# One scan instead of two for the diagonal tiles of stick-breaking attention, with zeros and the identity as the added operand

## The chip, the cores and the metric

The kernel runs on one core of one Trainium2 chip, as one launch for the whole layer. The metric is the time of an execution on the device, in microseconds. The core has five engines that run on their own queues and wait for each other: TensorE (PE in the profile, its weight loads PEld), VectorE (DVE), ScalarE (ACT), GpSimd (POOL) and SyncE (SP), which here issues the DMA transfers.

## What is computed

One layer of a hybrid encoder over a prompt of 2048 frames and 64 frames of a running stream, in fp32. The layer has one input projection of the normalised input; a recurrent branch (RG-LRU), a pooling branch and stick-breaking attention of four heads of 64; one output projection; and a feed-forward part (SwiGLU). The part that matters here is the attention:

```python
def stick_breaking(q, k, v, q_pos, k_pos):
    z = jnp.einsum("bqhd,bkhd->bhqk", q, k)
    mask = k_pos[None, :] < q_pos[:, None]
    nl = jnp.where(mask, jnp.log1p(jnp.exp(z)), 0.0)
    ...                       # surv[k] = sum of nl[j] over j >= k
    attn = jnp.where(mask, jnp.exp(z - surv), 0.0)
    return jnp.einsum("bhqk,bkhd->bqhd", attn, v)
```

With om = sigmoid(-z) = 1 / (1 + exp(z)), the product C[k] of om[j] over the keys j from k to the last one before the query is what is left of the stick, and attn[k] = C[k+1] - C[k]. The kernel computes C and multiplies it with differences of neighbouring rows of v, which were stored beforehand.

## The kernel before, in words

The prompt is worked through in four groups of 512 frames. For each group there are dense units (input projections in three fp32r products, the recurrent branch, pooling, queries, keys and values of the next group) and attention units. The program merges both into one list by hand-set weights (the lists o0, o1, o3 and the numbers alag and aspan in line 3), marks the attention units with a priority, and a scheduler lays out the order of each engine's instructions when the program is built, by these priorities and by when it reckons operands ready. So two neighbouring lines of code needn't be neighbours in an engine's queue. Then come the output projection and the feed-forward part.

An attention unit of group g takes one head, one block c of 512 keys (c from g down to 0) and two tiles of 128 queries. ATT_units (L673) loads queries, keys and differenced values with SP, from DRAM scratch that the earlier units wrote (kscr, qscr, vscr). For each of the two tiles it calls att_qtile (L647): PE multiplies queries by keys into the PSUM tile z (L650, L651); ACT overwrites z by the sigmoid (L653); DVE makes C in SBUF by scans from the last column to the first. A scan computes state = om * state + added, column after column. Back in ATT_units PE transposes C in pieces of 128 columns (L705), ACT and DVE split the transposes into a high and a low part (L706, L707), and PE multiplies both by the values into av. att_out (L665) adds the value of the query's own frame and stores.

Off the diagonal (c < g) a tile has 512 columns and one scan (L661) with zeros as the added operand (one column of zeros, zero1, broadcast) and the carry of the block to its right as its start. On the diagonal (c = g) the tile of query tile qt has (qt + 1) * 128 columns. There the last dg = 128 columns have a scan of their own (L657) with the reversed identity as the added operand and 0.0 as its start: the state stays zero for the keys after the query, is set to one at the query's own position and is a product from there on. A second scan (L661) goes on over the remaining w - dg columns, from that scan's last value. The sample's tile (ATT_sample, L723) has 64 queries and 320 columns, with dg = 64, once for each head.

The identity comes by DMA in X_first (L836), and shift_consts (L394) makes DVE constants from it. X_first also computes the first group's row statistics on PE from sums that DVE and POOL add up (L864). Keys go through fin_ (L366): DVE scales them (L368) and splits them (L315), SP stores them to kscr (L324), and the attention of the next group loads them (L685). The recurrent branch has scans of its own (L579).

Of the kernel before, what the change touches and what calls it, by code (L numbers as in the profile page):

```python
# [3 lines left out]
def prm(n,d):  # L4
    return type(d)(PRM.get(n,d))
# [7 lines left out]
F32 = mybir.dt.float32  # L13
# [3 lines left out]
ALU = mybir.AluOpType  # L17
# [4 lines left out]
P = 128  # L22
# [11 lines left out]
GW = 512  # L34
# [15 lines left out]
def hybrid_layer(ctx: ExitStack, tc: tile.TileContext, x_all, x_t, w_in, w_out, w_gu, w_dn, par, gates, poolw,  # L50
                 gn2, ident_in, cache_k, cache_v, y, new_k, new_v, o_conv, o_lru, o_pool):
    nc = tc.nc
    act, dve, gp, pe, sp = nc.scalar, nc.vector, nc.gpsimd, nc.tensor, nc.sync
# [23 lines left out]
    def mm(out, lhsT, rhs, start, stop):  # L77
        pe.matmul(out, lhsT, rhs, start=start, stop=stop)  # L78
# [35 lines left out]
    ident = cp.tile([P, P], F32, name="ident")  # L114
# [279 lines left out]
    def shift_consts():  # L394
        dve.tensor_scalar(dm[:, 0:1], ident[:, 0:1], -1.0, None, ALU.mult)
        dve.tensor_tensor(dm[:, 1:], ident[:, :P - 1], ident[:, 1:], ALU.subtract)
        dve.tensor_copy(em[:, 0:1], ident[:, P - 1:])
        sp.dma_start(clast, cache_v[PAST - 1:PAST, :])
# [244 lines left out]
    pa = s_att.enter_context(tc.tile_pool(name="pa", bufs=2, side="right"))  # L643
    zero1 = pa.tile([P, 1], F32, name="zero1", bufs=1)
    gp.memset(zero1, 0.0)

    def att_qtile(q2, n, K, w, dg, carry):  # L647

        z = psum.tile([P, GW], F32, name="z", tag="z", bufs=prm("nz", 2))
        mm(z[:n, :w], q2[:, 0, :], K[:, :w], True, False)  # L650
        mm(z[:n, :w], q2[:, 1, :], K[:, :w], False, True)  # L651
        om = z
        act.activation(om[:n, :w], z[:n, :w], AF.Sigmoid, scale=-1.0)  # L653
        C = pa.tile([P, GW], F32, name="C", bufs=prm("b_C", 5))
        if dg:

            dve.tensor_tensor_scan(C[:n, w - dg:w][:, ::-1], om[:n, w - dg:w][:, ::-1], ident[:n, :dg][:, ::-1], 0.0,  # L657
                                   ALU.mult, ALU.add)
            w, carry = w - dg, C[:n, w - dg:w - dg + 1]
        if w:  # L660
            dve.tensor_tensor_scan(C[:n, :w][:, ::-1], om[:n, :w][:, ::-1], zero1[:n].to_broadcast([n, w]), carry,  # L661
                                   ALU.mult, ALU.add)
        return C, C[:n, 0:1]

    def att_out(av, h, n, q2, vsrc, dst):  # L665
# [7 lines left out]
    def ATT_units(g):  # L673
        us = []
        for h in range(NH):
            st = {}
            for c in range(g, -1, -1):
# [11 lines left out]
                def u(pr, h=h, c=c, st=st, ld=ld):  # L689
                    if pr == 0:  # L690
                        ld()
                        if c == g:
                            st["av"] = psum.tile([P, GW], F32, name="av", tag="av", bufs=1)
                    q2, av, K, V = st["q"], st["av"], st["K"], st["V"]
                    aTh = pa.tile([P, 4, 256], F32R, name="aTh", bufs=prm("b_aTh", 2))
                    aTl = pa.tile([P, 4, 256], F32R, name="aTl", bufs=prm("b_aTl", 2))
                    for qq in range(2):
                        qt = pr * 2 + qq
                        nk = 4 if c < g else qt + 1
                        dg = P if c == g else 0  # L700
                        at, st["carry"][qt] = att_qtile(q2[:, :, qt * P:(qt + 1) * P], P, K, nk * P, dg,
                                                        st["carry"][qt])
                        tp = ps_a()
                        for kt in range(nk):
                            pe.transpose(tp[:, kt, :], at[:, kt * P:(kt + 1) * P], ident)  # L705
                        act.copy(aTh[:, :nk, qq * P:(qq + 1) * P], tp[:, :nk, :])  # L706
                        dve.tensor_tensor(aTl[:, :nk, qq * P:(qq + 1) * P], tp[:, :nk, :],  # L707
                                          aTh[:, :nk, qq * P:(qq + 1) * P], ALU.subtract)
                    nkt = 4 if c < g else 2 * pr + 2
                    for kt in range(nkt):  # L710
                        q0 = P if c == g and kt == 2 * pr + 1 else 0
                        o = av[:, pr * 256 + q0:pr * 256 + 256]
                        mm(o, V[:, kt, :], aTh[:, kt, q0:], c == g and kt == 0 and pr == 0, False)
                        mm(o, V[:, kt, :], aTl[:, kt, q0:], False, c == 0 and kt == nkt - 1 and pr == 1)
                    if c == 0 and pr == 1:
                        att_out(av, h, GW, q2, vtscr[g], mix[g])
# [6 lines left out]
    def ATT_sample(h):  # L723
        n, w = NS, PAST + NS
        q2 = pa.tile([P, 2, GW], F32R, name="q2", bufs=prm("b_q2", 2))
        for e in range(2):
            sp.dma_start(q2[e * HD:e * HD + HD, :, :n].bitcast(F32), qscr_s[h])
        K = pa.tile([P, GW], F32R, name="K", bufs=prm("b_K", 2))
        sp.dma_start(K[:, :w].bitcast(F32), kscr_s[h])
        V = pa.tile([P, 4, P], F32R, name="V", bufs=prm("b_V", 2))  # L730
        sp.dma_start(V[:, :2, :].bitcast(F32), vscr_s[:PAST, h, :].rearrange("(t p) e -> p t e", p=P))
        sp.dma_start(V[:NS, 2, :].bitcast(F32), vscr_s[PAST:, h, :])
        av = psum.tile([P, GW], F32, name="av", tag="av", bufs=1)
        at, _ = att_qtile(q2[:, :, :n], n, K, w, NS, 0.0)
        tp = ps_a()
        aTh = pa.tile([P, 4, 256], F32R, name="aTh", bufs=prm("b_aTh", 2))
        aTl = pa.tile([P, 4, 256], F32R, name="aTl", bufs=prm("b_aTl", 2))
        for kt, m in ((0, P), (1, P), (2, NS)):
            pe.transpose(tp[:m, kt, :n], at[:n, kt * P:kt * P + m], ident[:n, :n])
        for (m, a, b) in ((P, 0, 2), (NS, 2, 3)):  # L740
            act.copy(aTh[:m, a:b, :n], tp[:m, a:b, :n])
            dve.tensor_tensor(aTl[:m, a:b, :n], tp[:m, a:b, :n], aTh[:m, a:b, :n], ALU.subtract)
        for kt, m in ((0, P), (1, P), (2, NS)):
            mm(av[:, :n], V[:m, kt, :], aTh[:m, kt, :n], kt == 0, False)
            mm(av[:, :n], V[:m, kt, :], aTl[:m, kt, :n], False, kt == 2)
        att_out(av, h, n, q2, vtscr_s, mix_s)
# [68 lines left out]
    def X_first():  # L815
# [3 lines left out]
        for i in range(4):  # L819
# [10 lines left out]
            else:  # L830
# [4 lines left out]
        sp.dma_start(xs_, x_t[:, :, SEQ:].rearrange("k p t -> p k t"))  # L835
        sp.dma_start(ident, ident_in)  # L836
        shift_consts()
        acc = [psum.tile([P, 512], F32, name=t, tag=t, bufs=b) for t, b in
               (("tp", prm("ntp", 2)), ("tp", prm("ntp", 2)), ("z", prm("nz", 2)), ("z", prm("nz", 2)), ("av", 1))]
        sums = [pl.tile([P, SW], F32, name=t, tag=t, bufs=LB[t])[:, :GW] for t in ("r", "i")]  # L840
# [2 lines left out]
        for k in range(KD):  # L843
# [9 lines left out]
            w = slice((k % 4) * 256, (k % 4) * 256 + 256)  # L853
# [41 lines left out]
        for j, (ti, c0, n) in enumerate(toks(0)):  # L895
            with hp('ev'):
                ev_v(0, acc[j][:, :256], ti, c0, n, rss[:n, 0:1] if j == 4 else rs[1][:, j:j + 1])

    X_first()
    load_consts()  # L900
    if prm('cpos', 0) == 0:
# [475 lines left out]
```

## Time and profile before

| | us |
|---|---|
| median of three runs | 2429.84 |
| lowest and highest | 2428.33, 2432.44 |
| the profiled execution | 2430.59 |
| its span in the trace | 2428.8 |

| engine | busy us | share of the span |
|---|---|---|
| PE | 2315.6 | 95% |
| PEld | 2204.5 | 91% |
| DVE | 1561.7 | 64% |
| POOL | 1112.7 | 46% |
| ACT | 965.6 | 40% |

Busy times are read from the trace of one execution. The span is the trace's own length; the profiled execution's time is 1.8 us longer. Matmuls overlap in PE's pipeline, so that a busy PE isn't PE at its peak; the weight loads (PEld) show better how densely it is fed. The share of a whole span hides the stages: attention and the dense units run from 170 to 840 us, what follows is the output projection and the feed-forward part.

### The profile page before, as it was taken

Reading aid. Unit: us, or ns where it says so; the run is one execution under the profiler, and the core shown is the slowest. Engines: PE = TensorE matmul, PEld = TensorE weight load, DVE = VectorE, ACT = ScalarE, POOL = GpSimd, SP = SyncE. Lnnn points to the kernel's source line nnn. Section 1 sums busy time; section 2 is a strip of 40 time slices with the busy share of each in tenths; the row PEclk is TensorE's granted clock in tenths of the full one; section 3 lists DMA queues with packets and bytes.
Section 4 is the critical chain, followed back from the end, with each engine's and each line's share of the span. In section 5 each row is a group of like instructions: output and inputs, shape, how many; then the busy total and the mean of one; then the engine's idle time right before and its main releaser. Section 6 shows DMA issues by size and latency. Waiting matters only on the chain.

```text
span 2428.8 us, 38577 instructions
## 1 busy us (share of the span) xinstructions
PE 2315.6 (95%) x14230; PEld 2204.5 (91%) x14230; DVE 1561.7 (64%) x2514; ACT 965.6 (40%) x1804; POOL 1112.7 (46%) x818
## 2 busy tenths in 40 slices
PE   6987999999889989889999999999999999999999
PEld 6976778779678989889999999999999999999999
DVE  4568486796798644696676768655554655555455
ACT  4545364464565422233333343334333433333332
POOL 4533030131131133576565666656565765655552
PEclk8999999999999999999999999999999999999999
DMA  8986777656546354774343348633333563333332
GB/s 281 262 280 197 222 219 225 192 192 206 170 150 175 104 146 129 250 233 131 113 139 118 123 147 267 237 105 122 109 108 114 160 214 108 118 112 108 115 110 74
DMA packets 228478, 399.90 MB, mean 165 GB/s; under 512 B 37697, under 2 KB 99714, under 8 KB 220354
## 3 DMA queue, kind: packets, MB, share of 16 engines
q1 hardware_dynamic: 228290, 397.44, 52.6%
q8 instruction: 112, 1.84, 0.3%
q14 instruction: 76, 0.62, 0.1%
HBM read 300.81 MB, written 96.54 MB: 164 GB/s over the span
## 4 chain that ended last, share of the span: by engine, by line
PE 72%; DVE 12%; DMA 9%; issue 3%; ACT 2%; SPq 1%; POOL 1%; DVEq 0%; ACTq 0%; POOLq 0%
PE gu L78 33%; PE dn L78 20%; PE mm L78 14%; PE z L78 2%; PE av L78 2%; DVE C L661 1%; PE tp L705 1%; DMA rb<-xrow 1%; DMA kscr<-hl 1%; PE tp L78 1%; DVE xc L533 1%; DMA rbk<-row 1%; DMA x1all<-xr 1%; DMA wk<-w 1%; DVE al L1226 1%
## 5 line engine op out<-in xcount | busy, mean ns | idle before, releaser
L86 POOL TENSOR_TENSOR w<-x,w 128x512 fp32r<-128x512 f32 x462 | 640.7, 1401 | 509.7 <-ACT w L1103 478.4
L78 PE MATMUL dn<-ah,wd 128*128 128x352 f32 x2112 | 548.0, 324 | 5.4 <-ACT ah L1225 3.4
L78 PE MATMUL gu<-ht,w 128*128 128x352 f32 x2112 | 545.8, 323 | 7.3 <-DVE u L1180 7.1
L1103 ACT CAST w<-x 128x512 fp32r<-128x512 f32 x462 | 279.0, 619 | 521.2 <-PE gu L78 295.8
L78 PE MATMUL mm<-hTh,w 128*128 128x512 f32 (+3 forms) x1632 | 431.2, 342 | 13.7 <-DVE xr L1005 7.3
L78 PE MATMUL gu<-hb,w 128*128 128x352 f32 x1584 | 417.3, 325 | 9.0 <-DMA x<-in_w_gu 7.3
L1256 DVE TENSOR_TENSOR acc<-dn,acc 128x352 f32<-128x352 f32 x528 | 273.1, 522 | 217.5 <-PE dn L78 216.9
L78 PEld LDWEIGHTS dn<-ah,wd 128*128 128x128 f32 x2112 | 376.4, 189 | 7.6 <-ACT ah L1225 4.2
L78 PEld LDWEIGHTS gu<-ht,w 128*128 128x128 f32 x2112 | 375.1, 188 | 8.9 <-issue 5.9
L78 PE MATMUL dn<-al,wd 128*128 128x352 f32 x1056 | 342.4, 324 | 3.3 <-DVE al L1226 3.3
L78 PE MATMUL gu<-lt,w 128*128 128x352 f32 x1056 | 341.0, 323 | 0.0
L78 PEld LDWEIGHTS mm<-hTh,w 128*128 128x128 f32 x1632 | 290.2, 194 | 44.3 <-DVE xr L1005 8.5
L78 PEld LDWEIGHTS gu<-hb,w 128*128 128x128 f32 x1584 | 284.1, 189 | 11.1 <-ACT w L1103 9.5
L78 PE MATMUL mm<-hTl,w 128*128 128x512 f32 (+3 forms) x816 | 277.6, 341 | 0.8 <-DVE hTl L303 0.4
L78 PE MATMUL gu<-lb,w 128*128 128x352 f32 x792 | 257.1, 325 | 0.0
L86 POOL TENSOR_TENSOR wd<-x,wd 128x512 fp32r<-128x512 f32 x132 | 192.4, 1478 | 51.6 <-ACT wd L1244 51.6
L78 PEld LDWEIGHTS dn<-al,wd 128*128 128x128 f32 x1056 | 199.7, 189 | 4.5 <-DVE al L1226 4.5
L78 PEld LDWEIGHTS gu<-lt,w 128*128 128x128 f32 x1056 | 198.6, 188 | 0.0
L78 PEld LDWEIGHTS mm<-hTl,w 128*128 128x128 f32 x816 | 157.8, 193 | 15.7 <-issue 1.4
L661 DVE TENSOR_TENSOR_SCAN C<-z,C,zero 128x512 f32<-128x512 f32 (+4 forms) x148 | 160.6, 1087 | 13.9 <-ACT z L653 7.5
L1180 DVE TENSOR_TENSOR u<-gu,u 128x352 f32<-128x352 f32 x132 | 68.9, 522 | 129.1 <-PE gu L78 128.8
L78 PEld LDWEIGHTS gu<-lb,w 128*128 128x128 f32 x792 | 150.0, 189 | 0.0
(272 smaller groups left out, 3540.5 us busy)
## 6 DMA issues: line engine op xcount, KB each, us to landing
x<-in_w_gu SPq DMA_DIRECT2D x220, 256.0 KB, 3.3
w<-wk SPq DMA_DIRECT2D x46, 1024.0 KB, 5.7
x<-wsc SPq DMA_DIRECT2D x176, 256.0 KB, 3.4
x<-in_w_dn SPq DMA_DIRECT2D x132, 256.0 KB, 2.8
wsc<-x SPq DMA_DIRECT2D x88, 256.0 KB, 2.7
wk<-w SPq DMA_DIRECT2D x16, 1024.0 KB, 9.1
V<-vscr SPq DMA_DIRECT2D x40, 256.0 KB, 3.8
K<-kscr SPq DMA_DIRECT2D x40, 256.0 KB, 3.6
```

Of the source, the lines that this page charges most:

```text
L78: pe.matmul(out, lhsT, rhs, start=start, stop=stop)
L86: gp.tensor_tensor(out, src, hi, ALU.subtract)
L533: dve.scalar_tensor_tensor(xc[:, a:b], xa[:, s + j:s + j + b - a], pv("cw", c * 4 + j), xc[:, a:b], ALU.mult, ALU.add)
L661: dve.tensor_tensor_scan(C[:n, :w][:, ::-1], om[:n, :w][:, ::-1], zero1[:n].to_broadcast([n, w]), carry, ALU.mult, ALU.add)
L705: pe.transpose(tp[:, kt, :], at[:, kt * P:(kt + 1) * P], ident)
L1103: act.copy(w[:, 0, :], src)
L1180: add = lambda o, x, y: dve.tensor_tensor(o, x, y, ALU.add)
L1226: dve.tensor_tensor(al[:, cs], o, ah[:, cs], ALU.subtract)
L1256: dve.tensor_tensor(acc[:, d, a:b], ps[:, :HT], acc[:, d, a:b], ALU.add)
```

## The change

A new constant tile zident of 128 x 512 holds 384 columns of zeros followed by the 128 x 128 identity. POOL sets the zeros at the start of the program; DVE copies the identity into it once its DMA has landed, after shift_consts. In att_qtile a tile has one scan over all its w columns. On the diagonal the added operand is the window of zident that ends at the identity's column dg and is w columns wide, read in reverse, and the start is the carry that the caller gives, which is 0.0 there. Off the diagonal the scan is as before.

```diff
+    zident = pa.tile([P, GW], F32, name="zident", bufs=1)
+    gp.memset(zident[:, :GW - P], 0.0)
     def att_qtile(q2, n, K, w, dg, carry):
...
         C = pa.tile([P, GW], F32, name="C", bufs=prm("b_C", 5))
-        if dg:
-
-            dve.tensor_tensor_scan(C[:n, w - dg:w][:, ::-1], om[:n, w - dg:w][:, ::-1], ident[:n, :dg][:, ::-1], 0.0,
-                                   ALU.mult, ALU.add)
-            w, carry = w - dg, C[:n, w - dg:w - dg + 1]
-        if w:
-            dve.tensor_tensor_scan(C[:n, :w][:, ::-1], om[:n, :w][:, ::-1], zero1[:n].to_broadcast([n, w]), carry,
-                                   ALU.mult, ALU.add)
+
+        add = zident[:n, GW - P + dg - w:GW - P + dg] if dg else zero1[:n].to_broadcast([n, w])
+        dve.tensor_tensor_scan(C[:n, :w][:, ::-1], om[:n, :w][:, ::-1], add[:, ::-1] if dg else add, carry, ALU.mult, ALU.add)
         return C, C[:n, 0:1]
...
         shift_consts()
+        dve.tensor_copy(zident[:, GW - P:], ident)
```

## Rows read from the trace of the kernel before

**Rows 1.** The page, part 1: engine, busy us, share of the span, instructions.

```profile
PE 2315.6 (95%) x14230; PEld 2204.5 (91%) x14230; DVE 1561.7 (64%) x2514; ACT 965.6 (40%) x1804; POOL 1112.7 (46%) x818
```

**Rows 2.** Busy times by stretch: length, PE, PEld, DVE, ACT, POOL (instructions), clock, DMA share, GB/s.

```profile
170.00:840.00 670.00, 622.54 (x3530) 528.68 (x3530) 508.64 (x805) 349.60 (x643) 132.17 (x90) 0.96 0.62 190
...
660.00:740.00 80.00, 71.76 (x394) 57.53 (x394) 72.88 (x104) 52.85 (x89) 24.17 (x13) 0.93 0.50 154
740.00:840.00 100.00, 98.32 (x771) 94.51 (x771) 83.16 (x120) 51.96 (x104) 11.13 (x14) 1.00 0.49 136
...
843.00:2428.00 1585.00, 1546.76 (x9784) 1538.01 (x9782) 960.17 (x1512) 540.53 (x1028) 904.32 (x664) 0.99 0.45 142
```

**Rows 3.** DVE's scans by shape, 170 to 835 us: busy us, mean ns, idle before.

```profile
L661 DVE TENSOR_TENSOR_SCAN C<-z,C,zero 128x512 f32<-128x512 f32 x96 | 122.2, 1275 | 13.2 <-ACT z L653 7.5 <-PE tp L705 4.8
...
L657 DVE TENSOR_TENSOR_SCAN C<-z,ident 128x128 f32<-128x128 f32 x64 | 25.9, 412 | 7.5 <-ACT z L653 7.5
...
L579 DVE TENSOR_TENSOR_SCAN r<-d,hlru,i 128x512 f32<-128x512 f32 x14 | 17.9, 1278 | 0.1
L661 DVE TENSOR_TENSOR_SCAN C<-z,C,zero 128x384 f32<-128x384 f32 x16 | 16.1, 1008 | 0.2
L661 DVE TENSOR_TENSOR_SCAN C<-z,C,zero 128x256 f32<-128x256 f32 x16 | 11.8, 741 | 0.2
...
L661 DVE TENSOR_TENSOR_SCAN C<-z,C,zero 128x128 f32<-128x128 f32 x16 | 7.6, 473 | 0.1
```

**Rows 4.** The chain in order of time, first and last second scan of fourteen: start, us.

```profile
185.44 0.10 DVE C L661
...
721.94 0.75 DVE C L661
```

**Rows 5.** Timeline of DVE around two diagonal tiles: start us, us, instruction.

```profile
197.57 0.41 DVE L657 TENSOR_TENSOR_SCAN C<-z,ident 128x128 f32<-128x128 f32 x1
...
200.98 0.75 DVE L661 TENSOR_TENSOR_SCAN C<-z,C,zero 128x256 f32<-128x256 f32 x1
...
758.18 0.42 DVE L657 TENSOR_TENSOR_SCAN C<-z,ident 128x128 f32<-128x128 f32 x1 [1.18 <-ACT z L653]
758.64 0.75 DVE L661 TENSOR_TENSOR_SCAN C<-z,C,zero 128x256 f32<-128x256 f32 x1
759.31 0.86 DVE L707 TENSOR_TENSOR aTl<-tp,aTh 128x512 fp32r<-128x512 f32 x2
```

**Rows 6.** PE's waits for C, 170 to 840 us (total, times, longest), and two of them.

```profile
PE tp L705 <- DVE C L661: 9.8, 10, 4.1
...
186.52 1.09 PE L705 MATMUL tp<-ident,C 128*128 128x128 f32 x4 [4.12 <-DVE C L661]
...
201.88 0.52 PE L705 MATMUL tp<-ident,C 128*128 128x128 f32 x3 [1.78 <-DVE C L661]
```

**Rows 7.** Timeline of the start: POOL's memset and first tensor operation; DVE and PE.

```profile
1.35 0.21 POOL L390 MEMSET em<- 128x128 f32 x1
...
7.12 1.04 POOL L860 TENSOR_TENSOR i<-q 128x512 f32<-128x512 f32 x1 [5.29 <-DMA q<-in_x_t]
...
24.50 0.28 DVE L396 TENSOR_TENSOR dm<-ident 128x127 f32<-128x127 f32 x1
...
24.70 0.14 DVE L397 COPY em<-ident 128x1 f32<-128x1 f32 x1
...
25.59 0.60 PE L78 MATMUL mm<-ones,r 128*128 128x1 f32 x2 [0.27 <-DVE r L864]
```

**Rows 8.** Chain: a key store and a key load; PE's waits, 430-465 and 636-665 us.

```profile
447.25 7.67 DMA kscr<-hl
...
655.82 3.35 DMA K<-kscr
...
PE z L78 <- DMA K<-kscr: 1.6, 1, 1.6
...
PE z L78 <- DMA K<-kscr: 4.3, 1, 4.3
```

## The prediction

> **What bounds the kernel now.** I read the page first: PE is busy for 95% of the span, DVE for 64% [rows 1]. That is an average over unlike stages, so I next took the busy times by stretch [rows 2]. From 843 us to the end the weight loads fill 1538.0 of 1585 us: that part is bound by PE, and the change has no instruction in it. The diagonal scans all lie between 170 and 840 us, where attention runs beside the projections. There PE's weight loads fill 528.7 of 670 us (79%) and DVE 508.6 (76%): neither is full, and in the stretch from 660 to 740 us DVE is at 72.9 of 80 us (91%) while the weight loads are at 57.5 (72%). So in this stage the end is carried in turn by PE, by DVE, by ACT and by DMA, and a saving on DVE counts only where the chain passes through DVE. The third view was therefore the chain that ended last, read window by window for the scans on it [rows 4], and the fourth the timeline of DVE around some diagonal tiles, for what stands between the two scans of one tile [rows 5].
>
> **What is removed.** For a diagonal tile of width w the kernel runs a 128-column scan (L657) and then, from its last value, a scan over the other w - 128 columns (L661). There are 64 diagonal tiles of prompt queries and 4 of the sample; 16 of the 64 have w = 128 and have one scan before and after. So 48 + 4 = 52 instructions go, and no column: the fused scan runs over the same w.
>
> The price of a scan [rows 3]: from 741 to 1008 to 1275 ns is 267 ns for 128 columns each time, so an L661 scan is about 207 ns plus 267 per 128 columns, and an L657 scan is 412 - 267 = 145 ns plus the same. The two forms differ in two things, the added operand (a broadcast zero or the full identity) and the start value (a column of C or the constant 0.0). The lane scan of L579 has a full added operand and a column as its start and takes 1278 ns for 512, as much as L661 with the broadcast; so the full operand costs nothing and the 62 ns are the column. The fused scan has a full operand and a constant start, as L657 has: 145 + 267 per 128 columns, that is 679, 946 and 1213 ns for w = 256, 384 and 512. The pairs now take 412 + 473 (207 + 267 rounded), 412 + 741 and 412 + 1008. Each pair loses about 207 ns of busy time: 48 x 0.207 = 9.9 us, and with four sample tiles at about the same price 10.7 us of DVE's 508.6.
>
> Busy time isn't time in the queue. Neighbours on DVE overlap: the scan begun at 758.64 us lasts 0.75 and the next instruction starts at 759.31, 0.08 earlier than its end [rows 5]. Where other work lies between the two scans, both overlap their neighbours, and the pair costs the queue 0.207 - 0.08 = 0.13 us more than the fused scan. Where the second follows the first at once, it must wait for its start value: 758.18 to 759.39 us is 1.21 us against 0.946, a difference of 0.26. I take 0.21 per pair, the busy time, which lies between these ends; both kinds are common in DVE's timeline, and the tiles at 197.57 and 758.18 us stand for them [rows 5].
>
> [...]
>
> **What of it lies on the path.** In the chain between 170 and 840 us I count 14 of the 52 second scans; the one at 185.44 us is there for 0.10 us only [rows 4]. 13 x 0.21 = 2.7 us, with ends of 13 x 0.13 = 1.7 and 13 x 0.26 = 3.4. The other 39 lie beside work that ends later (PE's projections, DMA round trips, ACT); there the gain is slack. Both far ends stand as bounds: none of the 10.7 us on the path, or all of it.
>
> **What is added.** A memset of 384 columns on POOL: 128 columns take 0.21 us there, so about 0.6 us. POOL then sits idle for 5.29 us until its first tensor operation at 7.12 us, so it costs nothing; if that cover were gone, 0.6 [rows 7]. A DVE copy of the identity, 128x128. It is queued where DVE's small operations on the identity run (0.14 us for one column, 0.28 for 127 columns with two inputs), directly ahead of the sum that PE waits for at 25.59 us [rows 7]; behind it on DVE are that sum and everything for the first row statistics. I put it at 0.2 us on the path, with ends 0.1 and 0.3. The fused scan waits for nothing new after that. It is also a longer block that nothing can enter, 1.21 us at most, but off the diagonal DVE already runs 96 blocks of 1.275 us [rows 3], so the queue meets no new size of block. The added tile lies in the pool whose room a later stage takes over; a diagonal tile is read before the tiles left of it, so it isn't the last to be given up.
>
> The sum: -2.7 + 0.2 = -2.5 us. The profiled execution took 2430.59 us (span 2428.8 and 1.8 around it), so it would take 2428.1; it lies 0.75 above the median of 2429.84, and the median would be **2427.3 us**, 0.1% less.
>
> **What can go otherwise.** The order on each engine is set when the program is built, and not by the order in the code: the scan of 197.57 us has its second half at 200.98, with work of other units between them [rows 5], while at 758 us nothing stands between. With 52 instructions fewer the order may be laid out anew from the first diagonal tile on.
>
> *Rival 1, a larger gain.* Where other work stands between the two scans, C is now complete late, and PE's transposes wait for it: ten such waits, 9.8 us, the longest 4.12 us before 186.52; one of the ten belongs to a tile off the diagonal and is worth 0.5 [rows 6]. A fused scan begun when the first one begins now would be done after its 0.68 to 1.21 us. At 201.88 it would be done at 198.25 instead of 201.73, and the wait of 1.78 would be gone; before 186.52 it shortens the wait by 1.7. Reckoned so for the nine, each capped by its wait, it is 6.0 us, and the median would be 2429.8 + 0.2 - 6.0 = 2424.0. In its favour: these are real idle times of PE. Against it: the work that now stands between moves behind the scan, and among it is the split of the next group's input (L301), for which PE's projections wait. If all 10.7 us of DVE counted, 2419.3.
>
> *Rival 2, hidden.* The chain closes again over PE, ACT and DMA, and only the copy remains: 2430.0. For it: DVE idles some 160 of the 670 us, and from 740 to 840 us, where much of the last group's attention runs, the weight loads are at 94.5 of 100 us [rows 2]. Against it: 13 scans on the chain. [...]
>
> *Rival 3, slower: a hand-over of keys is laid bare.* The keys of the next group go from DVE through a store (7.67 us at 447.25) and a load (3.35 us at 655.82) before PE can start on the group [rows 8]; PE now waits 1.6 us for it at the second hand-over and 4.3 at the third. If, in the new order, attention reaches the second hand-over sooner or DVE's split of the keys is put later, up to 7.67 + 3.35 - 1.6 = 9.4 us more of it shows: 2427.3 + 9.4 = 2436.7. It decides from 7.4 us on, where the loss exceeds the gain of 2.5 and a further 4.9 us, 0.2%. For it: a chain that already passes through these transfers at each hand-over. Against it: less work on DVE makes the split of the keys earlier, not later, unless the order changes.
>
> That the fused scan is no cheaper than the pair is all but excluded by L657 and L579, which have its two operand forms.
>
> **How the numbers follow.** Forecast (2.5 us less, 1.4 to 3.3) 0.38; rival 1 0.33; rival 2 0.13; rival 3 0.16. A difference under 0.2%, 4.9 us, is about what a measurement of this kernel can tell from no change. The forecast and rival 2 lie within it, rival 1 beyond it on the fast side, rival 3 on the slow one: faster 0.33, same 0.51, slower 0.16. The range reaches on the fast side to rival 1 with all of DVE's saving (2419) and on the slow side to nearly the whole of rival 3 (2436).
>
> **What would show it.** The profile after should have 164 scans on one line: 96 of 128x512 at 1.275 us, and 16 each of 412, 679, 946 and 1213 ns, with DVE's scan time down by some 10.7 us in all. On the forecast PE's idle time in 170 to 840 us shrinks by two or three us; with rival 1 the transposes' waits for C drop from 9.8 to under 4; with rival 2 the scans shrink and the out-projection starts where it did; with rival 3 a wait for K over 9 us appears at a hand-over. I am wrong at the root if a fused scan takes over 1.3 us, or if the stretch after 843 us changes its length.

## The result, and the profile after

The changed kernel takes 2444.59 us (median of six runs, 2441.78 to 2449.4); the kernel before took 2429.09 on the same chip (six runs, 2426.21 to 2432.44). The ratio is 1.0065, 95% interval 1.0051 to 1.0078: 15.5 us slower, where 2.5 us faster was forecast and the range ended at 2436. The profiled execution of after is the slowest of its six, 2449.4 us with a span of 2447.6.

The scans did what the prediction said. The first rows are part 1 of the page of after (as [rows 1]), then VectorE's groups by line and shape from 170 to 850 us (as [rows 3]: busy us, mean ns, idle before). Lines of attention stand one to two lower than before: the scan is L660, the sigmoid L656, the transposes L703.

```profile
PE 2328.2 (95%) x14230; PEld 2211.6 (90%) x14230; DVE 1570.0 (64%) x2463; ACT 963.9 (39%) x1804; POOL 1105.1 (45%) x819
```

```profile
L660 DVE TENSOR_TENSOR_SCAN C<-z,C,zero 128x512 f32<-128x512 f32 x96 | 122.2, 1275 | 13.4 <-PE tp L703 7.1 <-ACT z L656 5.1
L533 DVE SCALAR_TENSOR_TENSOR xc<-xa,par_sb,xc 128x512 f32<-128x512 f32 x41 | 39.5, 963 | 4.1 <-ACT xc L531 3.7
L660 DVE TENSOR_TENSOR_SCAN C<-z,zident 128x512 f32<-128x512 f32 x16 | 19.4, 1212 | 3.6 <-ACT z L656 3.5
...
L660 DVE TENSOR_TENSOR_SCAN C<-z,zident 128x384 f32<-128x384 f32 x16 | 15.1, 945 | 2.5 <-ACT z L656 2.5
L568 DVE SCALAR_TENSOR_TENSOR sqt<-r,d 128x512 f32<-128x512 f32 x12 | 11.1, 923 | 1.5 <-ACT r L565 1.5
L660 DVE TENSOR_TENSOR_SCAN C<-z,zident 128x256 f32<-128x256 f32 x16 | 10.8, 675 | 0.2 <-ACT z L656 0.2
...
L660 DVE TENSOR_TENSOR_SCAN C<-z,zident 128x128 f32<-128x128 f32 x16 | 6.7, 416 | 1.6 <-ACT z L656 1.6
```

The fused scans take 416, 675, 945 and 1212 ns; 412, 679, 946 and 1213 were worked out. On the prompt's diagonal tiles that is 52.0 us of VectorE instead of 61.4. Yet VectorE's busy time didn't fall by the removed scans: it rose, from 1561.7 [rows 1] to 1570.0 us, with 51 instructions fewer. So other instructions got longer. Two of them, in the same view of the kernel before (170 to 840 us), had these means; after, they have 963 and 923 ns:

```profile
L533 DVE SCALAR_TENSOR_TENSOR xc<-xa,par_sb,xc 128x512 f32<-128x512 f32 x40 | 34.3, 857 | 4.0 <-ACT xc L531 3.7
...
L568 DVE SCALAR_TENSOR_TENSOR sqt<-r,d 128x512 f32<-128x512 f32 x12 | 8.3, 691 | 0.1
```

Where the time went is best seen by the time at which TensorE has begun a given number of matmuls. This table is worked out from the matmul records of the two traces, counted from the start and interpolated between steps of 2 us. The two orders don't issue the same matmuls at the same count, so a lag is good to some 3 us.

| matmuls | before, us | after, us | lag |
|---|---|---|---|
| 870 | 166.7 | 164.0 | -2.7 |
| 1070 | 215.8 | 226.8 | 11.0 |
| 1300 | 264.4 | 272.1 | 7.7 |
| 2050 | 415.8 | 424.8 | 9.0 |
| 3200 | 642.0 | 650.5 | 8.5 |
| 3300 | 670.6 | 680.8 | 10.2 |
| 3600 | 730.5 | 749.2 | 18.7 |
| 4380 | 834.9 | 850.2 | 15.3 |
| end of the span | 2428.8 | 2447.6 | 18.8 |

Most of the loss is made at two places: between the 870th and the 1070th matmul, where the attention of the first group begins, and between the 3200th and the 3600th, where that of the last group does. Elsewhere the lag moves by 3.5 us at most.

**The first place.** TensorE's waits from 150 to 225 us (total, times, longest), first before, then after:

```profile
PE tp L705 <- DVE C L661: 5.9, 2, 4.1
PE mm L78 <- ACT i L558: 2.5, 1, 2.5
PE mm L78 <- ACT hTh L302: 0.8, 1, 0.8
...
PE z L78 <- DMA K<-kscr: 0.3, 1, 0.3
```

```profile
PE tp L703 <- DVE C L660: 5.2, 3, 3.4
PE z L78 <- DMA K<-kscr: 3.8, 1, 3.8
PE mm L78 <- ACT hTh L302: 3.2, 2, 2.9
PE mm L78 <- DVE sqt L308: 2.1, 2, 1.7
```

Waits for the keys, for the split of the next group's input (L302) and for the projections' scaling (L308) are 9.1 us after and 1.1 before; against that the wait for L558, 2.5 us, is gone, and that for C is 0.7 shorter. So the waits are not the whole of the loss. From the 870th to the 1070th matmul the two traces show:

| | length, us | TensorE busy | idle | granted clock |
|---|---|---|---|---|
| before, 166.7 to 215.8 us | 49.1 | 38.7 | 10.4 | 0.93 |
| after, 164.0 to 226.8 us | 62.8 | 47.0 | 15.8 | 0.84 |

Both stretches hold 202 matmul records. Of the 13.7 us, 5.4 are idle time and 8.3 are matmuls that take longer, at a lower granted clock; that the clock is the reason is argued from these rows, not tested.

The keys come later because VectorE's split of them (L315) stands later in its queue, and the store follows it. Timelines (start, length in us, instruction): before, VectorE and then the DMA queue,

```profile
158.04 0.68 DVE L315 TENSOR_TENSOR hl<-raw,hl 128x512 fp32r<-128x512 f32 x1
```

```profile
161.74 1.32 SPq L324 DMA_DIRECT2D kscr<-hl  x2
```

and after, VectorE, the DMA queue and TensorE:

```profile
173.09 0.68 DVE L315 TENSOR_TENSOR hl<-raw,hl 128x512 fp32r<-128x512 f32 x1
```

```profile
173.80 1.25 SPq L324 DMA_DIRECT2D kscr<-hl  x2
```

```profile
183.38 1.19 PE L78 MATMUL z<-K,q 128*128 128x128 f32 x4 [3.82 <-DMA K<-kscr]
```

No attention scan is between these instructions. The queues were laid out differently long before: SyncE's order parts from that of the kernel before at its 14th instruction (10.07 us before, 10.77 after), ahead of the copy's own time of 25.64 us, and VectorE's ten instructions behind the copy (28.99 before, 30.50 after).

**The second place.** VectorE, GpSimd and TensorE between 709 and 730 us, after:

```profile
709.40 1.28 DVE L705 TENSOR_TENSOR aTl<-tp,aTh 128x512 fp32r<-128x512 f32 x2
710.60 5.20 DVE L533 SCALAR_TENSOR_TENSOR xc<-xa,par_sb,xc 128x512 f32<-128x512 f32 x2
...
723.56 2.37 DVE L568 SCALAR_TENSOR_TENSOR sqt<-r,d 128x512 f32<-128x512 f32 x1 [0.29 <-ACT r L565]
725.85 0.68 DVE L705 TENSOR_TENSOR aTl<-tp,aTh 128x512 fp32r<-128x512 f32 x1
726.45 2.53 DVE L569 SCALAR_TENSOR_TENSOR d<-sqt,d 128x512 f32<-128x512 f32 x1
```

```profile
709.95 2.38 POOL L86 TENSOR_TENSOR w<-stg,w 128x1024 fp32r<-128x1024 f32 x1 [11.36 <-ACT w L970]
712.90 2.34 POOL L86 TENSOR_TENSOR w<-stg,w 128x1024 fp32r<-128x1024 f32 x1 [0.58 <-ACT w L970]
...
722.98 2.40 POOL L86 TENSOR_TENSOR w<-stg,w 128x1024 fp32r<-128x1024 f32 x1 [1.26 <-ACT w L970]
726.04 2.38 POOL L86 TENSOR_TENSOR w<-stg,w 128x1024 fp32r<-128x1024 f32 x1 [0.67 <-ACT w L970]
```

```profile
715.85 3.78 PE L78 MATMUL mm<-xc,gw 128*128 128x512 f32 x4 [3.78 <-DVE xc L533]
```

The two steps of L533, 1.5 us for two where nothing stands beside them, take 5.20 beside GpSimd's two subtractions; L568 and L569 take 2.37 and 2.53 beside the next two. The pair of L533, L568 and L569 each end 0.55 us behind the end of a subtraction (715.80 against 715.24, 725.93 against 725.38, 728.98 against 728.42), as if each had waited for the subtraction and then run; that is a reading of these times, which no run tests by itself. TensorE waits 3.78 us for xc. The subtractions make the low part of w_out (line 974); an experiment below takes them away. The stretch from 640 to 760 us, before and then after (columns as [rows 2]): 619 matmuls against 521 in the same 120 us, with VectorE equally busy.

```profile
640.00:760.00 120.00, 106.07 (x619) 87.72 (x619) 102.63 (x153) 76.19 (x131) 29.34 (x19) 0.94 0.57 175
```

```profile
640.00:760.00 120.00, 99.52 (x521) 78.32 (x521) 102.51 (x136) 68.62 (x113) 25.01 (x15) 0.91 0.50 153
```

### The profile page after: what moved, and what is told of

Read it like the earlier page. It is cut to its first block, busy times and chain, and to the rows that moved or that the text cites. A ratio compares the mean times of both kernels' runs of the same rounds, so it can differ in the third digit from the quotient of the medians.

```text
span 2447.6 us, 38500 instructions
## 1 busy us (share of the span) xinstructions
PE 2328.2 (95%) x14230; PEld 2211.6 (90%) x14230; DVE 1570.0 (64%) x2463; ACT 963.9 (39%) x1804; POOL 1105.1 (45%) x819
## 4 chain that ended last, share of the span: by engine, by line
PE 71%; DVE 13%; DMA 10%; issue 3%; ACT 2%; SPq 1%; POOL 1%; DVEq 0%; ACTq 0%; POOLq 0%
PE gu L78 33%; PE dn L78 19%; PE mm L78 13%; DVE C L660 2%; PE z L78 2%; PE av L78 2%; PE tp L703 1%; DVE xc L533 1%; DMA rbk<-row 1%; DVE aTl L705 1%; PE tp L78 1%; DMA kscr<-hl 1%; DMA mix<-r 1%; DVE r L579 1%; DMA stg<-mix 1%
## 5 line engine op out<-in xcount | busy, mean ns | idle before, releaser
L78 PE MATMUL mm<-hTh,w 128*128 128x512 f32 (+3 forms) x1632 | 440.3, 347 | 20.1 <-DVE xr L1004 7.6
L78 PEld LDWEIGHTS mm<-hTh,w 128*128 128x128 f32 x1632 | 295.4, 198 | 52.2 <-DVE xr L1004 8.6
L1225 DVE TENSOR_TENSOR al<-s,ah 128x352 fp32r<-128x352 f32 x132 | 125.6, 953 | 26.0 <-ACT ah L1224 20.6
```

The costliest lines, as they stand in the source:

```text
L1225: dve.tensor_tensor(al[:, cs], o, ah[:, cs], ALU.subtract)
```

## The experiments

Each ratio is to runs of the kernel before on the same chip (its median there 2420.5 to 2421.9 us), with a 95% interval. "Older order" is the order in which each engine issues in the kernel before, "newer order" that of the changed kernel. An order is fixed by a recorded list for each engine, in which every instruction is chained to the one ahead; it adds no wait on a semaphore:

```diff
         hybrid_layer(tc, *args)
+        pin_order(tc, nc)
```

**The fused scan in the older order.** All of the change, with the fused scan where the second scan stood (e1_second):

> The changed kernel, with every engine held to the issue order of the kernel before (ordering edges without semaphores; the fused scan stands where the second scan stood, the copy and the memset behind the instructions that they follow in the code). Theory A, the order: the loss of 15.5 us comes only from the order that the scheduler laid out anew, so it is gone, and what is left is DVE's saving on the path, 2 to 4 us: 2425 to 2428. Theory B, the fused scan itself: a block of up to 1.21 us that nothing can enter, with a full added operand, delays what queues behind it; then the loss stays, 2440 to 2446. Theory C, the copy and the memset at the start cost it: the loss stays as well.

and where the first scan stood (e1_first):

> As the kernel above, but the fused scan stands where the first of the two scans stood, so C is complete earlier and the work that lay between the two scans moves behind it. Rival 1 of the prediction, tested without a new order: PE's nine waits for C shrink by 6.0 us, so 2422 to 2425, faster than with the scan in the second place. If the work moved behind it matters as much as C, the two are alike, 2425 to 2429. Theories B and C: 2440 to 2446.

Measured: 0.9999 (0.9987 to 1.001) and 1.0018 (1.001 to 1.0027). In the order of the kernel before the change costs nothing, as theory A had it; the saving of 2 to 4 us that it expected doesn't show in this run. Beginning the scan earlier is no gain but a small loss, which no theory had. TensorE's waits from 170 to 850 us fit that; first the run with the scan at the second place, then at the first:

```profile
PE tp L703 <- DVE C L660: 8.4, 10, 2.6
PE z L78 <- DVE C L660: 7.9, 13, 1.6
```

```profile
PE z L78 <- DVE C L660: 11.4, 14, 2.6
...
PE tp L703 <- DVE C L660: 4.2, 4, 2.7
```

The transposes' waits halve, as the prediction's first rival had it, but other waits take their place: those of the products z, which need a scan to have read the earlier z, grow by 3.5 us, and what stood between the two scans now stands behind the fused one.

**The newer order without the change.** The kernel before, its two scans side by side, in the newer order, with no copy and no memset (e2_two_scans_after_order); and the kernel before with the memset and the copy, which nothing reads, its order laid out freely (e3_copy_alone):

```diff
+    zident = pa.tile([P, GW], F32, name="zident", bufs=1)
+    gp.memset(zident[:, :GW - P], 0.0)
...
         shift_consts()
+        dve.tensor_copy(zident[:, GW - P:], ident)
```

> The kernel before, two scans and neither copy nor memset, with every engine held to the issue order of the changed kernel (the two scans stand one behind the other in the place of the fused one). Theory A: the order alone brings the loss, and the dearer scans add 2 to 5 us: 2445 to 2450. Theories B and C: back at the time of the kernel before, 2427 to 2432.

> The kernel before with the memset and the copy added and nothing reading their tile; two scans as before, the order left to the scheduler. It separates the two causes of a new order. If the copy at the start is what turned the order over (the trace of the changed kernel is 9 to 10 us behind before its first diagonal scan), this one is 7 to 15 us slower than before, 2436 to 2444. If the removed scans did it, it stays at 2427 to 2432. Theory B: 2427 to 2432.

Measured: 1.0080 (1.0062 to 1.0098) and 1.0028 (1.0017 to 1.004). The order alone makes the whole loss. The changed kernel's 1.0065 is 0.15% under it, but the two intervals overlap. A copy of 0.21 us and a memset of 0.41 us that nothing reads cost 6.8 us, where 7 to 15 were expected; the cost isn't their own time, since e1_second has both in the older order and loses nothing. The order of e3_copy_alone parts from that of the kernel before at the same instructions of SyncE and VectorE as the changed kernel's. Which of the two, copy or memset, turns it over wasn't tried.

**The change without the copy**, its order laid out freely (e4_no_copy):

```diff
-    ident = cp.tile([P, P], F32, name="ident")
...
     zident = pa.tile([P, GW], F32, name="zident", bufs=1)
     gp.memset(zident[:, :GW - P], 0.0)
+    ident = zident[:, GW - P:]
...
-        dve.tensor_copy(zident[:, GW - P:], ident)
```

> The changed kernel without the copy of the identity: the identity lands by DMA in the last 128 columns of zident, and the constants read it there. The order is laid out freely when the program is built. Theory (the copy at the start is what turns the order over): the order stays near that of the kernel before and the time within 0.15% of it, ratio 0.9985 to 1.001. Rival (the scans' removal turns the order over as well, wherever it starts): an order with a time of its own, over 0.2% away on either side.

Measured: 1.0025 (1.0016 to 1.0034), as the rival had it. The copy isn't the only thing that turns the order over: the edit without it gets an order of its own, 6 us slower than the kernel before and 9.7 faster than the changed kernel.

**Where in the order.** Kernels with the changed kernel's instructions, whose order is the older one as far as a point and the newer one behind it, or the reverse. The point is the first attention scan, or TensorE's 1300th or 3300th instruction. By the matmul records of h3 to h6 the 1300th comes at some 256 to 268 us and the 3300th at 660 to 677. So the second point lies just behind the last group's first loads of keys, and not ahead of them at 640 us as the expectations say.

> The instructions of the changed kernel. Every engine issues in the order of the kernel before as far as the first attention scan (about 180 us) and from there on in the order of the changed kernel. Theory (two places of loss, the first made by the order ahead of the first scan): the first loss is gone and the one after the third hand-over of keys stays, 7 to 11 us over the kernel before, ratio 1.003 to 1.0045. Rival (the order behind the first scan makes all of it): 13 to 17 us, as the changed kernel, 1.0055 to 1.007.

> The same the other way round: the changed kernel's order as far as the first attention scan, then the order of the kernel before. Theory: only the first loss, 6 to 9 us over the kernel before, ratio 1.0025 to 1.004. Rival: no loss, within 2 us, 0.999 to 1.001.

> The instructions of the changed kernel, in the order of the kernel before as far as PE's 3300th instruction (about 640 us, ahead of the third hand-over of keys), then in the changed kernel's order. Theory (two places): only the second loss, which the counts of matmuls done put at about 10 us: 8 to 11 us over the kernel before, ratio 1.0035 to 1.0045. Rival (the second loss is a consequence of what was late at the first place): within 3 us, 0.999 to 1.0015.

> The same the other way round: the changed kernel's order as far as PE's 3300th instruction, then the order of the kernel before. Theory: only the first loss, 6 to 9 us over the kernel before, ratio 1.0025 to 1.004; with h3 it adds up to the 15 us of the changed kernel. Rival: all of the loss, 13 to 17 us, 1.0055 to 1.007.

> The instructions of the changed kernel, in the order of the kernel before as far as PE's 1300th instruction (about 255 us, behind the first hand-over of keys), then in the changed kernel's order. Theory (the order around the first hand-over makes the first loss, and the second follows from it): within 4 us of the run with the older order to 3300, ratio 0.996 to 0.9995. Rival (the changed kernel's order between 255 and 640 us makes the loss): 1.004 to 1.007.

> The instructions of the changed kernel, in its own order as far as PE's 1300th instruction (about 260 us), then in the order of the kernel before; the mirror of the run with the older order to 1300. Theory (each place makes a loss of its own: the first some 9 us by the waits for keys and the input's split ahead of 215 us, the second by VectorE's instructions beside GpSimd's subtractions of w_out): only the first loss, ratio 1.0025 to 1.0045, and between 640 and 745 us no VectorE instruction at lines 533, 568 and 569 over 2 us. Rival (the second is a consequence of what was late at the first): as the changed kernel, ratio 1.0055 to 1.008, with such instructions.

| order up to the first scan | on to 1300 | on to 3300 | behind | ratio |
|---|---|---|---|---|
| older | older | older | older | 0.9999 (0.9987 to 1.001), again 0.9984 (0.9974 to 0.9995) |
| newer | older | older | older | 1.0008 (0.9996 to 1.0021), h2 |
| older | newer | newer | newer | 1.0061 (1.0048 to 1.0075), h1 |
| newer | newer | older | older | 1.0024 (1.0009 to 1.0039), h6 |
| older | older | newer | newer | 1.0025 (1.0015 to 1.0035), h5 |
| newer | newer | newer | older | 1.0098 (1.0082 to 1.0114), h4 |
| older | older | older | newer | 0.9967 (0.9953 to 0.998), h3; again 0.9973 (0.9963 to 0.9984) |
| newer | newer | newer | newer | 1.0065 (1.0051 to 1.0078), after |

Pairs of rows that differ in one column give what the newer order costs there. Up to 1300: 0.32% (h6 against the mean of the first row, 0.9992) and 0.40% (after against h5). From 1300 to 3300: 0.74% (h4 against h6) and 0.55% (h5 against the mean of h3's two, 0.9970). Behind 3300: a gain, 0.22% (h3 against the first row) and 0.33% (after against h4). Each price was taken twice, with the other parts of the order older and with them newer, and the two agree within their intervals; so a part costs about the same whatever the rest is, and one of them is a gain. (That the prices add up to the whole, 1.0065 - 0.9992, follows from how the pairs are chosen and shows nothing.)

Of the six expectations only h6's came near (1.0024, where 1.0025 to 1.0045 was expected), and of its two signs one failed: no VectorE instruction at L533, L568 and L569 was to take over 2 us, but L569 takes 2.78 at 700.44 us. h1 and h2 came out as their rivals; h3, h4 and h5 lie outside both ranges. The order ahead of the first scan was to make the first loss and costs only 0.04% (after against h1) to 0.16% (h2 against the first row), though h2 shows a longer wait ahead of the first attention product than the changed kernel does, 7.2 us, put down to a store of the stream's keys; h1, with the older order up to that point, shows none and waits for the input's split instead (150 to 225 us, h2, then h1):

```profile
PE z L78 <- DMA kscr_s<-hl: 7.2, 1, 7.2
```

```profile
PE mm L78 <- ACT hTh L302: 8.8, 2, 8.6
```

And the second loss comes to light around and behind the 3300th matmul but is made by the order ahead of it: h4, which has the older order from there on, has it in full (L533 takes 5.11 us for two), and h3, which has the newer one, has not.

The lag against the kernel before, counted as in the table of the result, shows the two places in each run. Its growth is, one trace each:

| run | 870th to 1070th | 1070th to 3200th | 3200th to 3600th |
|---|---|---|---|
| after | 13.7 | -2.5 | 10.2 |
| h4 (newer to 3300) | 10.7 | -2.9 | 13.4 |
| h6 (newer to 1300) | 12.7 | -9.7 | -0.3 |
| h5 (newer from 1300) | 0.7 | -1.8 | 3.9 |
| h3 (newer from 3300) | 0.6 | -4.1 | -1.0 |
| e1_second (older) | 1.4 | -5.3 | -2.0 |
| e4_no_copy (an order of its own) | -1.5 | -1.4 | 8.4 |

So neither loss needs the other: h6 has the first alone, e4_no_copy the second alone. What a lag costs at the end also depends on what follows: h6 regains most of its 12.7 us in the older order behind it. In h5 L568 and L569 take 2.38 and 2.49 us, as after, yet the lag grows by 3.9 us only; that a drawn-out instruction costs what waits for it fits this, but isn't shown by it.

**What the second loss is.** In the newer order (e7_after_nosplit) and in the older one (e7_before_nosplit), GpSimd's eight subtractions for the low part of w_out are memsets; this part of the weights is then zero.

```diff
-            rest(lo, hi, st)
+            gp.memset(lo.bitcast(F32), 0.0)
```

> The changed kernel in its own order, but GpSimd's eight subtractions for the low part of w_out (line 974) are memsets of that part to zero, so that the low part of w_out is left out. Theory (the second loss is VectorE's instructions drawn out beside these subtractions, 5.1 us for two of 0.75 at line 533, and the waits of TensorE behind them): 5 to 9 us under the changed kernel, ratio to the kernel before 1.003 to 1.0045. Rival (the second loss comes from elsewhere): within 2 us of the changed kernel, 1.0055 to 1.0075.

> The same edit with the fused scans in the order of the kernel before (as e1_second). Theory: VectorE has little beside the subtractions there, so 0 to 3 us under e1_second, ratio 0.9985 to 1.0. Rival (the subtractions cost as much in any order): 5 to 9 us, ratio 0.9965 to 0.998.

Measured: 1.0018 (1.0007 to 1.003), down from 1.0065 and below the range expected, and 0.9984 (0.9972 to 0.9997), against 0.9999 and 0.9984 without the edit. In the newer order the subtractions cost 0.47%, some 11 us; in the older one, with the same instructions, 0 to 0.15%. In the newer order's trace without them the lag grows by 12.9 us at the first place and by 1.2 at the second, where it grew by 10.2. VectorE's timeline in the newer order without the subtractions shows the instructions of 5.20, 2.37 and 2.53 us at their own length, 7.2 us less in all; then GpSimd's memsets of that time:

```profile
704.37 1.53 DVE L533 SCALAR_TENSOR_TENSOR xc<-xa,par_sb,xc 128x512 f32<-128x512 f32 x2
711.86 0.69 DVE L568 SCALAR_TENSOR_TENSOR sqt<-r,d 128x512 f32<-128x512 f32 x1 [0.35 <-ACT r L565]
713.07 0.68 DVE L569 SCALAR_TENSOR_TENSOR d<-sqt,d 128x512 f32<-128x512 f32 x1
```

```profile
709.98 2.12 POOL L974 MEMSET w<- 128x1024 f32 x2
```

The edit also frees the staging buffers sooner, since nothing waits for ScalarE's cast there, so not all of the 11 us need be the overlap.

**Is the first loss the same?** Two subtractions of GpSimd stand behind it too, those of the value weights: 5.20 us at 215.06, with VectorE's L575 at 2.57 us beside them. They are memsets in e8_after_novsplit (newer order) and e8_before_novsplit (older), so that the low part of these weights is left out:

```diff
+                elif key is not None and key[0] == 2:
+                    gp.memset(lo.bitcast(F32), 0.0)
                 else:
                     rest(lo, hi, st)
```

> The changed kernel in its own order, but GpSimd's two subtractions for the low part of the value weights (reached from line 451; 5.20 us at 215.06 us) are memsets to zero, so that this low part is left out. Theory (the first loss too is VectorE's instructions drawn out beside GpSimd's: 2.57 us at line 575 and 2.13 at line 301 beside these two, and TensorE's wait of 3.38 us for C there): 3 to 6 us under the changed kernel, ratio to the kernel before 1.004 to 1.0053. Rival (the first loss is the keys' late split, or VectorE's work that the order puts ahead of 215 us): within 2 us of the changed kernel, 1.0055 to 1.0075.

> The same edit with the fused scans in the order of the kernel before. There the same two subtractions take 5.70 us at 213.32 us. Theory: 0 to 2 us under the run without the edit, ratio 0.998 to 0.9995. Rival (they cost as much in any order): 3 to 6 us under it, 0.9965 to 0.998.

Measured: 1.0068 (1.0055 to 1.0081) and 0.9994 (0.9982 to 1.0005). Nothing is gained in either order, so the first loss isn't this; in the newer order's trace the lag still grows by 16.4 us at the first place. What remains for it are the waits and the longer matmuls shown above, by the rows alone.

**A version faster than both.** h3 (the older order to the 3300th instruction, the newer behind it) was run again, beside the older order throughout and beside h3's order with the two scans of the kernel before and without copy and memset:

> The version that was faster than both kernels, once more, beside the fused scans in the older order throughout: the older order as far as PE's 3300th instruction, then the changed kernel's. If the gain is real, ratio 0.9955 to 0.998; if it was the chip's, 0.9985 to 1.001.

> The fused scans in the order of the kernel before throughout, once more, on the chip of the run above: ratio 0.9985 to 1.001. If the order behind the 3300th instruction is what gains, the run above is 0.2 to 0.4% under it.

> The kernel before with its two scans, no copy and no memset, in the order of the version that was faster than both; the second scan directly behind the first. Theory (the order makes the difference, the fused scan adds 0 to 4 us): ratio 0.9967 to 0.9985. Rival (in this order VectorE is the bound, and all of the scans' 10.7 us count): 1.0 to 1.0015.

Measured: 0.9973 (0.9963 to 0.9984), 0.9984 (0.9974 to 0.9995) and 0.9997 (0.9986 to 1.0008). With its first run, 0.9967, the version is 0.3% faster than the kernel before, some 7 us. Most of it is the scans' here: with two scans the same order gives 0.9997, 0.24% more, which lies between the theory's range and the rival's. The intervals of the first two overlap, so that by these two runs the order behind 3300 is worth something between nothing and 0.3%; after against h4, 0.33%, speaks for a gain.

## Why the prediction was wrong

**The terms of the sum held.** 52 instructions went, 10.7 us of VectorE were forecast to go, and the prompt's tiles alone lost 9.4. The copy took 0.21 us in its place (0.2 forecast) and the memset 0.41 ahead of an idle GpSimd (0.6). What the scans are worth on the path, 2.7 us by the chain, was measured by pairs of kernels in one order: 0.01 and 0.16% in the older order, 0.15% in the newer (after against e2), 0.24% in h3's. The mean, 0.14%, is 3.4 us, with the copy's 0.2 in it in all four; from the intervals of the eight ratios it is good to some 0.08%, 2 us. So 2.5 us fits; of the four, the second and the last are clear of noise by themselves.

**The step that failed was the path they were laid on.** The sum took every other instruction to stay where it was. The prediction saw that the order "may be laid out anew from the first diagonal tile on", and priced this only in rivals 1 and 3. It is laid out anew from the start of the program, SyncE's from 10 us and VectorE's from 29 us on, where the first scan is at 174.5, and by either part of the edit: the copy and the memset alone move the time by 6.8 us, the change without the copy by 6, all of it together by 15.5. The changed kernel's loss is that of one order against another, 0.73%, with the scans' gain taken off it.

**Rival 1** (a larger gain) fell: with the scan begun at the first place the transposes' waits for C went from 8.4 to 4.2 us and the time rose by 0.2%. The objection that the prediction itself raised fits: what stood between the scans moved behind them, and other waits took the place of those for C.

**Rival 2** (hidden) and the forecast aren't told apart by the two runs in the older order, at 0.01 and 0.16% of gain; h3's order speaks for the forecast, while the newer order's 0.15% isn't clear of noise.

**Rival 3** (a hand-over of keys laid bare) named the right kind of event, at the wrong place and with too small a chance, 0.16; that its price, up to 9.4 us, is of the size of the loss there is chance. The prediction looked at the second and the third hand-over, where TensorE already waited 1.6 and 4.3 us [rows 8]; it was the one ahead of them, of the first group's own keys, where it had waited 0.3. The keys' split stands 15 us later and the wait is 3.8 us, not over 9 as the prediction's sign for this rival had it. And h2 has a wait of 7.2 us there and loses 0.16% against the older order, some 4 us, so the wait for keys is not by itself the loss. What else is in it is known by the rows only: 5.4 us of idle time in all and 8.3 us of longer matmuls. The experiments show that the order up to the 1300th instruction makes it, and that the subtractions of the value weights don't.

**The second loss was in no rival.** The rows for it were in the trace of the kernel before, where L569 takes 2.79 us at 704.74 and one step of L533 1.58 at 696.42, beside GpSimd's subtractions (VectorE, then GpSimd, before):

```profile
696.42 1.58 DVE L533 SCALAR_TENSOR_TENSOR xc<-xa,par_sb,xc 128x512 f32<-128x512 f32 x1
697.93 1.27 DVE L661 TENSOR_TENSOR_SCAN C<-z,C,zero 128x512 f32<-128x512 f32 x1
...
704.74 2.79 DVE L569 SCALAR_TENSOR_TENSOR d<-sqt,d 128x512 f32<-128x512 f32 x1
```

```profile
695.09 5.15 POOL L86 TENSOR_TENSOR w<-stg,w 128x1024 fp32r<-128x1024 f32 x2 [7.79 <-DMA stg<-in_w_out]
...
704.46 5.28 POOL L86 TENSOR_TENSOR w<-stg,w 128x1024 fp32r<-128x1024 f32 x2 [0.77 <-ACT w L971]
```

The prediction read GpSimd's work as cover for the memset alone and asked nowhere what VectorE's instructions cost beside it.

In the trace of after, L568, whose two inputs are both in SBUF, takes 2.37 us beside a subtraction of 2.40, while the pair of L705 at 709.40, with one input in PSUM, takes 1.28 us beside one of 2.38. Whether the place of the inputs makes this difference, no run tests.

**What the prediction said would show it wrong at the root** did not come: no fused scan takes over 1.3 us, and the stretch behind the 4380th matmul takes 1597.4 us after and 1593.9 before, a difference that the spread of either kernel's six runs, 6 to 8 us, covers. The prediction had no sign for a loss ahead of that stretch other than a wait for keys.

What stays open is which instructions between the 1300th and the 3300th of TensorE's set the second loss up, and what share of the first loss each wait has and the lower clock.

## What to carry to other kernels

Where a scheduler lays out the queues when the program is built, a forecast that keeps the order covers only part of what an edit does: here one order against another is worth 0.7% and the edit itself some 0.14%. To learn what an edit is worth, pin the order of the kernel before and change the instructions alone; then treat the order as a change of its own, cut it into stretches and take each from where it is better. In a trace look for VectorE instructions that take several times their own mean, and see what GpSimd does at that moment.

## What the chip showed that was not expected

- VectorE instructions of 0.75 and 0.69 us took 2.4 to 2.6 us each beside a GpSimd subtraction of 2.3 to 2.4 us, while a scan beside such subtractions wasn't drawn out (in the trace of before 1.27 us at 697.93, beside two subtractions of 5.15 us from 695.09 on; the mean of the 96 is 1275 ns in both kernels). Eight subtractions cost some 11 us in one order and 0 to 3.6 in another.
- A part of the order had about the same price whatever the other parts were: 0.32 and 0.40% up to the 1300th matmul instruction, 0.74 and 0.55% on to the 3300th, -0.22 and -0.33% behind it.
- At the first place the loss was more than the waits. After, TensorE was busy for 1.2 of the 5 us from 180 to 185 us, and from 185 to 190 us its granted clock was 0.50. The kernel before fell there as well (busy for 1.7 us, then 0.50), but was back at 0.97 from 190 to 195 us, where after it was 0.72; and after it fell again to 0.66 from 215 to 220 us, behind 5 us with 2.3 busy. Over the whole place it was 0.84 against 0.93, and 202 matmul records were busy for 47.0 us, against 38.7 for 202.
